# Attention scores from 64-row matmuls, the two maps on the two halves of the array's rows

## The chip, the cores and the metric

The kernel runs on one core of a Trainium2 chip. The metric is the device time of one execution, in microseconds (us). Before the change three runs gave 1631.43, 1632.15 and 1634.57 us, a median of 1632.15 us. Times inside an execution come from one profiled execution of the kernel before.

## What is computed

One layer of a hybrid encoder on 1024 tokens of width 1024, in float32. The change is in the differential attention branch: 4 heads, each with two score maps (m = 0 and 1) over 64-wide queries and keys, and one 128-wide value. Cut to that, the reference is:

```python
qa = apply_rope(qa.reshape(B, S, DA_HEADS, 2, DA_QK_DIM), cos, sin)
ka = apply_rope(ka.reshape(B, S, DA_HEADS, 2, DA_QK_DIM), cos, sin)
...
s = jnp.einsum('bqhmd,bkhmd->bhmqk', q_blk, k).astype(jnp.float32) * scale
s = jnp.where(mask, s, -jnp.inf)
a = jax.nn.softmax(s, axis=-1)
w = a[:, :, 0] - lam * a[:, :, 1]
return jnp.einsum('bhqk,bkhe->bqhe', w.astype(v.dtype), v)
```

Queries go in blocks of 128, and a block sees the keys up to its own end (64-wide chunks are masked causally). An mLSTM branch, gates, an output projection, a gated MLP and a per-layer embedding follow; the change does not touch them.

## The kernel before, in words

**Precision.** TensorE works on float32 operands that are rounded on entry (type fp32r), so each operand x is split into a rounded part hi and a rest lo = x - hi, and a product is the sum of three matmuls, hi·hi + hi·lo + lo·hi. `split` (L119) makes the two parts: hi on ScalarE (L121), lo on VectorE (L122). A 1024-deep projection is `gemm_part` (L144): per 128 rows of depth, three matmuls (L150, L151, L152) of 128 columns of weights by 512 tokens.

**The attention stage.** It runs from about 62 to 345 us of the span. Per head `make_q`, `make_k` and `make_va` (L594 to L623) project the queries, keys and values, 8 steps of 6 matmuls each. `rope_evict` (L572) takes a projected half (512 tokens) from PSUM, swaps its 32-row groups with four small DMAs on SP's queue (L581), and turns it (L582 to L584, VectorE). Rows 0 to 63 of the result (`UP`) belong to map 0 and rows 64 to 127 (`DN`) to map 1. The inner functions `parts` then split it:

- Queries: q0 holds the hi part of map 0 on the upper rows and its lo part on the lower rows, q1 the same for map 1 the other way round (L599 to L602: two ScalarE copies and two VectorE subtractions of 64 partitions for each half).
- Keys: k0 holds map 0's hi part on both halves of the rows, k1 map 1's, and kl both lo parts (L612 to L617: two ScalarE copies, two VectorE copies, two VectorE subtractions for each half).

So one 128-row matmul gives hi·hi + lo·hi of one map, and one 64-row matmul with kl gives hi·lo:

```python
PE.matmul(o, qs[h][m][:, qc], kk[m][:, n0:n1], start=True, stop=False)
PE.matmul(o, qs[h][m][r, qc], kl[r, n0:n1], start=False, stop=True)
```

These are L656 and L657 in `scores`. `weights(h, qb)` (L647) calls it for a block of 128 queries with nk = (qb+1)·128 keys, in chunks of up to 512 keys. Blocks with nk of 512 or less (qb 0 to 3) write both maps into one PSUM tile of two banks (`big`, of which there are two). Wider blocks (qb 4 to 7) take one such tile for each map, the second after the first map's scores. Then come the mask (L667, L680), the row maximum (L668, L681) on VectorE and the exponential with its row sum on ScalarE (L660). `transposed` (L687) joins the two maps (L694), turns them over on TensorE (L700) and copies them out (L701); `values` (L704) multiplies by the values (L708).

**What sets the order.** The loop at L733 writes a block's scores one block ahead of its transposes and values, and pulls single projection steps of the following heads (and later of the mLSTM values, `ps_v`) between them: one after the scores, two after the transposes. This written order gives the priorities; the framework that builds the program then arranges each engine's queue, and an instruction whose buffer or operand is not ready lets others pass it at build time. On the chip each engine keeps the order that came out. Queries and keys live in a ring of nine [128 x 1024] buffers (`qk_tile`, `NQK`), five of them for a head.

Of the kernel before, what the change touches and what calls it, by code (L numbers as in the profile page):

```python
# [11 lines left out]
F32 = mybir.dt.float32  # L12
F32R = mybir.dt.float32r
AF = mybir.ActivationFunctionType
ALU = mybir.AluOpType
# [7 lines left out]
HALF = 512  # L23
# [46 lines left out]
def block_kernel(ctx: ExitStack, tc: tile.TileContext, a: dict, out: bass.AP):  # L70
    nc = tc.nc
    PE, ACT, DVE, POOL, SP = nc.tensor, nc.scalar, nc.vector, nc.gpsimd, nc.sync
# [37 lines left out]
    def big(name):  # L110
        return pools["big"].tile([P, S], F32, tag="big", name=name)
# [7 lines left out]
    def split(hi, lo, src, scale=None, lo_eng=None):  # L119
        if scale is None:  # L120
            ACT.activation(out=hi, in_=src, func=AF.Copy)  # L121
            (lo_eng or DVE).tensor_tensor(out=lo, in0=src, in1=hi.bitcast(F32), op=ALU.subtract)  # L122
        else:
            ACT.activation(out=hi, in_=src, func=AF.Copy, scale=scale)
            DVE.scalar_tensor_tensor(
                out=lo, in0=src, scalar=scale, in1=hi.bitcast(F32), op0=ALU.mult, op1=ALU.subtract)
# [112 lines left out]
    def z_tile(t, name, evict):  # L239

        if t in ahead:
            for half, ps in enumerate(ahead.pop(t)):
                evict(half, half_slice(half), ps)
            return
        load_z(t)
        w = z_w.pop(t)
        z_order.remove(t)
        wide = big(name) if t == T_VA else None
        for half in range(2):
            if half and z_order:  # L250
                load_z(z_order[0])
            c = half_slice(half)
            ps = acc(name) if wide is None else wide[:, c]
            for k in range(0, KD, Z_STEP):
                last = k + Z_STEP == KD
                gemm_part(w[k:k + Z_STEP], cut(xg[k:k + Z_STEP], c), ps, first=k == 0, last=last)
                if last:
                    evict(half, c, ps)
                yield
# [286 lines left out]
    with tc.tile_pool(name="att", bufs=1) as at:  # L546
# [20 lines left out]
        UP, DN = slice(0, 64), slice(64, 128)  # L567

        def qk_tile(name):
            return at.tile([P, S], F32R, tag="qk", name=name, bufs=NQK)  # L570
# [15 lines left out]

            return evict

        def sub(out, in0, in1, eng=DVE):
            eng.tensor_tensor(out=out, in0=in0, in1=in1.bitcast(F32), op=ALU.subtract)  # L590

        qs, ks, vas = {}, {}, {}

        def make_q(h):  # L594

            q0, q1 = qs[h] = qk_tile("q0"), qk_tile("q1")

            def parts(rt, c):
                ACT.activation(out=q0[UP, c], in_=rt[UP, c], func=AF.Copy)  # L599
                ACT.activation(out=q1[DN, c], in_=rt[DN, c], func=AF.Copy)  # L600
                sub(q0[DN, c], rt[UP, c], q0[UP, c])
                sub(q1[UP, c], rt[DN, c], q1[DN, c])  # L602

            yield from z_tile(T_Q + h, "ps_q", rope_evict(0.125, parts))

        def make_k(h):

            k0, k1, kl = qk_tile("k0"), qk_tile("k1"), qk_tile("kl")
            ks[h] = (k0, k1), kl

            def parts(rt, c):
                ACT.activation(out=k0[UP, c], in_=rt[UP, c], func=AF.Copy)  # L612
                ACT.activation(out=k1[DN, c], in_=rt[DN, c], func=AF.Copy)
                DVE.tensor_copy(out=k0[DN, c], in_=k0[UP, c].bitcast(F32))
                DVE.tensor_copy(out=k1[UP, c], in_=k1[DN, c].bitcast(F32))
                sub(kl[UP, c], rt[UP, c], k0[UP, c])
                sub(kl[DN, c], rt[DN, c], k1[DN, c])  # L617

            yield from z_tile(T_K + h, "ps_k", rope_evict(1.0, parts))

# [24 lines left out]
        acc4 = []  # L645
        if True:
            def weights(h, qb):  # L647
                kk, kl = ks[h]
                nk = (qb + 1) * P
                qc = slice(qb * P, (qb + 1) * P)  # L650
                rs = at.tile([P, 2], F32, tag="rsum", name="rsum", bufs=3)
                nm = at.tile([P, 2], F32, tag="nmax", name="nmax", bufs=3)

                def scores(o, m, n0, n1):
                    r = (UP, DN)[m]
                    PE.matmul(o, qs[h][m][:, qc], kk[m][:, n0:n1], start=True, stop=False)  # L656
                    PE.matmul(o, qs[h][m][r, qc], kl[r, n0:n1], start=False, stop=True)  # L657

                def expo(m, e, s_):
                    ACT.activation(out=e, in_=s_, func=AF.Exp, bias=nm[:, m:m + 1], scale=1.0,  # L660
                                   accum_out=rs[:, m:m + 1])

                if nk <= HALF:
                    ps = big("ps_s").rearrange("p (m k) -> p m k", m=2)
                    for m in range(2):
                        scores(ps[:, m, 0:nk], m, 0, nk)
                    DVE.memset(ps[0:CHUNK, :, nk - CHUNK:nk], NEG)  # L667
                    DVE.tensor_reduce(out=nm, in_=ps[:, :, :nk], axis=AX.X, op=ALU.max, negate=True)  # L668
                    et = at.tile([P, S], F32, tag="e", name="e", bufs=4)
                    es = [et[:, 0:nk], et[:, HALF:HALF + nk]]  # L670
                    for m in range(2):
                        expo(m, es[m], ps[:, m, :nk])
                else:
                    es = []
                    for m in range(2):
                        ps = big("ps_s")
                        for n0 in range(0, nk, HALF):
                            n1 = min(nk, n0 + HALF)
                            scores(ps[:, n0:n1], m, n0, n1)
                        DVE.memset(ps[0:CHUNK, nk - CHUNK:nk], NEG)  # L680
                        DVE.tensor_reduce(out=nm[:, m:m + 1], in_=ps[:, :nk], axis=AX.X, op=ALU.max, negate=True)  # L681
                        et = at.tile([P, S], F32, tag="e", name="e", bufs=4)
                        expo(m, et[:, :nk], ps[:, :nk])
                        es.append(et[:, :nk])
                return es, rs

            def transposed(es, rs, qb):  # L687

                rr = at.tile([P, 2], F32, tag="rr", name="rr", bufs=3)
                DVE.reciprocal(out=rr, in_=rs)  # L690
                cc = at.tile([P, 1], F32, tag="cc", name="cc", bufs=3)
                DVE.scalar_tensor_tensor(out=cc, in0=rs[:, 0:1], scalar=neglam, in1=rr[:, 1:2],
                                         op0=ALU.mult, op1=ALU.mult)
                DVE.scalar_tensor_tensor(out=es[0], in0=es[1], scalar=cc, in1=es[0], op0=ALU.mult, op1=ALU.add)  # L694
                wT = at.tile([P, S], F32, tag="wT", name="wT", bufs=2)
                for j0 in range(0, qb + 1, 4):
                    j1 = min(qb + 1, j0 + 4)
                    pt = mid("pt")
                    for j in range(j0, j1):
                        PE.transpose(pt[:, (j - j0) * P:(j - j0 + 1) * P], es[0][:, j * P:(j + 1) * P], ident)  # L700
                    ACT.activation(out=wT[:, j0 * P:j1 * P], in_=pt[:, :(j1 - j0) * P], func=AF.Copy)  # L701
                return es, rr, wT

            def values(h, qb, es, rr, wT):  # L704
                va = vas[h]
                pav = mid("pav")
                for j in range(qb + 1):
                    PE.matmul(pav[:, :P], wT[:, j * P:(j + 1) * P], va[:, j, :], start=(j == 0), stop=(j == qb))  # L708

                i = qb % 4  # L710
                if i == 0:
                    acc4[:] = [at.tile([P, 4, P], F32, tag="oh", name="oh", bufs=2),
                               at.tile([P, 4], F32, tag="s2", name="s2", bufs=2)]
                oh, s2 = acc4
                DVE.tensor_scalar(out=oh[:, i, :], in0=pav[:, :P], scalar1=rr[:, 0:1], scalar2=None, op0=ALU.mult)
                ACT.activation(out=es[0][:, 0:P], in_=oh[:, i, :], func=AF.Square, accum_out=s2[:, i:i + 1])
                if i == 3:
                    tails.append((h, oh, s2, qb // 4))
                if tails and i == 1:
                    norm_tail(*tails.pop())  # L720
# [73 lines left out]
    def work(name, w=S, dtype=F32):  # L794
        return mw.tile([P, w], dtype, tag="m", name=name)
# [187 lines left out]
    for n, j in enumerate(OUT_ORDER):  # L983
        i = j % 4
        m = work("mg")
# [4 lines left out]
        if n % 2 == 0:  # L990
            k1 = m
# [242 lines left out]
    with tc.tile_pool(name="fin", bufs=2) as fp:  # L1234
# [25 lines left out]
        for t0, t1 in PLE_CHUNKS:  # L1260
            n = t1 - t0
            c = slice(t0, t1)
# [109 lines left out]
```

## Time and profile before

| what | value |
|---|---|
| median of three runs | 1632.15 us |
| the profiled execution's own time | 1633.46 us |
| its span, first to last instruction | 1631.6 us |
| VectorE busy | 1253.8 us (77%) |
| ScalarE busy | 730.1 us (45%) |
| GpSimd busy | 23.4 us (1%) |
| weight loads of TensorE (PEld) busy | 1284.6 us (79%) |
| mean granted clock of TensorE | 0.984 |

Busy time counts an engine's own work, not what it waits for. Matmul records overlap in the pipeline, so TensorE's pace is better read from start to start than from the length of a record. A weight load (PEld) normally runs while the matmul before it streams. In a timeline row, the bracket at the end gives the idle time in front of the instruction and what ended it; "issue" means that nothing in the profile shows what it waited for.

### The profile page before, as it was taken

How to read it: one execution, taken by the hardware profiler on the slowest of the kernel's cores; microseconds unless marked ns; L12 is line 12 of the kernel's file. 1: busy time of each engine (PE TensorE's matmuls, PEld its weight loads, DVE VectorE, ACT ScalarE, POOL GpSimd, SP SyncE). 2: the span in 40 equal slices, each digit the busy share in tenths (PEclk: the TensorE clock that was granted, in tenths of full speed). 3: DMA queues.
4: the chain of work that ended last, by engine and by line, in shares of the span. 5: the costliest groups of instructions: out<-in, count | busy, mean ns of one | idle time of the engine just before them, and what ended most of it. 6: DMA issues, size and time to landing. Idle time of an engine off the chain costs nothing.

```text
span 1631.6 us, 20986 instructions
## 1 busy us (share of the span) xinstructions
PE 1576.9 (97%) x7317; PEld 1284.6 (79%) x7317; DVE 1253.8 (77%) x2208; ACT 730.1 (45%) x1412; POOL 23.4 (1%) x22
## 2 busy tenths in 40 slices
PE   8999999998899999998998999999999989999997
PEld 7767777776787788887886788888888768788997
DVE  6687685576878878759869978877787897878745
ACT  3354453554464664543446433333333544343522
POOL 0000000000000000000000000000000000000000
PEclk8999999999999999999999999999999999999998
DMA  5212121063334232355413332333333654442422
GB/s 187 72 27 71 40 71 41 27 222 117 125 102 127 81 131 92 117 191 164 155 47 134 110 103 98 103 107 101 102 106 102 207 182 148 143 134 58 133 83 91
DMA packets 97882, 181.62 MB, mean 111 GB/s; under 512 B 11696, under 2 KB 21488, under 8 KB 97776
## 3 DMA queue, kind: packets, MB, share of 16 engines
q1 hardware_dynamic: 97200, 179.76, 34.1%
q8 instruction: 58, 0.95, 0.2%
q10 hardware_dynamic: 576, 0.52, 0.1%
q14 instruction: 48, 0.39, 0.1%
HBM read 131.18 MB, written 44.86 MB: 108 GB/s over the span
## 4 chain that ended last, share of the span: by engine, by line
PE 64%; DVE 9%; issue 2%; DMA 2%; ACT 1%; POOL 0%; SPq 0%; POOLq 0%; DVEq 0%; ACTq 0%
PE b L376 18%; PE b L374 18%; PE b L375 18%; PE ps_pg L1272 1%; PE ps_pg L1273 1%; PE ps_pg L1274 1%; DVE cv L823 1%; DVE T L122 1%; DVE mg L292 1%; DVE wl L122 1%; DVE B L122 1%; PE ps_ya L152 1%; DVE hs L388 1%; DMA sg<-ya 1%; PE ps_ya L151 1%
## 5 line engine op out<-in xcount | busy, mean ns | idle before, releaser
L374 PE MATMUL b<-T,wh 128*128 128x512 f32 x816 | 320.0, 392 | 3.8 <-DVE x L292 1.4
L376 PE MATMUL b<-T,wl 128*128 128x512 f32 x816 | 319.8, 392 | 3.8 <-DVE wl L122 3.8
L375 PE MATMUL b<-T,wh 128*128 128x512 f32 x816 | 318.8, 391 | 0.5 <-DVE T L122 0.5
L121 ACT ACTIVATE wh<-S 128x512 fp32r<-128x512 f32 (+1 forms) x208 | 129.4, 622 | 275.6 <-PE b L375 249.1
L374 PE MATMUL b<-B,wh 128*128 128x512 f32 x612 | 240.7, 393 | 2.5 <-ACT wh L121 2.0
L376 PE MATMUL b<-B,wl 128*128 128x512 f32 x612 | 240.1, 392 | 0.6 <-DVE wl L122 0.6
L375 PE MATMUL b<-B,wh 128*128 128x512 f32 x612 | 239.8, 392 | 0.5 <-DVE B L122 0.5
L122 DVE TENSOR_TENSOR wl<-S,wh 128x512 fp32r<-128x512 f32 (+1 forms) x208 | 140.1, 674 | 61.0 <-ACT wh L121 61.0
L374 PEld LDWEIGHTS b<-T,wh 128*128 128x128 f32 x816 | 153.7, 188 | 40.4 <-DVE x L292 2.6
L376 PEld LDWEIGHTS b<-T,wl 128*128 128x128 f32 x816 | 153.8, 188 | 38.3 <-DVE wl L122 6.2
L375 PEld LDWEIGHTS b<-T,wh 128*128 128x128 f32 x816 | 153.8, 188 | 33.4 <-DVE T L122 1.6
L121 ACT ACTIVATE wh<-wr 128x512 fp32r<-128x512 f32 (+1 forms) x156 | 96.9, 621 | 166.6 <-PE b L375 151.6
L374 PEld LDWEIGHTS b<-B,wh 128*128 128x128 f32 x612 | 115.4, 189 | 27.6 <-ACT wh L121 3.3
L376 PEld LDWEIGHTS b<-B,wl 128*128 128x128 f32 x612 | 115.5, 189 | 25.4 <-DVE wl L122 1.7
L375 PEld LDWEIGHTS b<-B,wh 128*128 128x128 f32 x612 | 115.4, 189 | 25.3 <-DVE B L122 1.8
L292 DVE TENSOR_TENSOR x<-b,x 128x512 f32<-128x512 f32 x112 | 77.0, 688 | 47.9 <-PE b L376 46.4
L122 DVE TENSOR_TENSOR wl<-wr,wh 128x512 fp32r<-128x512 f32 (+1 forms) x156 | 104.9, 672 | 7.5 <-ACT wh L121 5.9
L292 DVE TENSOR_TENSOR S<-wr 128x512 f32<-128x512 f32 (+1 forms) x104 | 70.3, 676 | 1.7 <-DMA wr<-w_down 0.2
L1117 DVE SCALAR_TENSOR_TENSOR ac<-ar,vec,ac 128x511 f32<-128x511 f32 (+1 forms) x88 | 65.8, 747 | 0.7
L121 ACT ACTIVATE wh<-wf 128x512 fp32r<-128x512 f32 (+1 forms) x56 | 33.5, 601 | 63.0 <-PE ps_q L151 19.5
L1272 PE MATMUL ps_pg<-x,wpg 128*128 128x384 f32 (+1 forms) x192 | 61.3, 319 | 0.0
L1274 PE MATMUL ps_pg<-x,wpg 128*128 128x384 f32 (+1 forms) x192 | 61.0, 318 | 0.0
(305 smaller groups left out, 2794.8 us busy)
## 6 DMA issues: line engine op xcount, KB each, us to landing
wr<-w_up SPq DMA_DIRECT2D x88, 256.0 KB, 2.8
wr<-w_in SPq DMA_DIRECT2D x56, 256.0 KB, 3.0
wf<-w_in SPq DMA_DIRECT2D x32, 256.0 KB, 2.9
wr<-w_down SPq DMA_DIRECT2D x32, 256.0 KB, 2.8
xt<-xT SPq DMA_DIRECT2D x8, 512.0 KB, 6.2
sw<-raw SPq DMA_DIRECT2D x64, 64.0 KB, 2.0
hs<-xT SPq DMA_DIRECT2D x8, 512.0 KB, 5.4
ya<-ya SPq DMA_DIRECT2D x16, 256.0 KB, 2.0
```

The source lines that it names most:

```text
L121: ACT.activation(out=hi, in_=src, func=AF.Copy)
L122: (lo_eng or DVE).tensor_tensor(out=lo, in0=src, in1=hi.bitcast(F32), op=ALU.subtract)
L151: PE.matmul(ps, wh, xl, start=False, stop=False)
L152: PE.matmul(ps, wl, xh, start=False, stop=(last and k == n - 1))
L292: eng.tensor_tensor(out=out, in0=in0, in1=in1, op=op)
L374: PE.matmul(bank[b], wh, xh, start=(k == 0 and not more), stop=False, **kw)
L375: PE.matmul(bank[b], wh, xl, start=False, stop=False, **kw)
L376: PE.matmul(bank[b], wl, xh, start=False, stop=(k == n - 1), **kw)
L388: DVE.scalar_tensor_tensor(out=hs[i][:, c], in0=(src or hs)[i][:, c], scalar=v(gain, i), in1=rstd[:, c], op0=ALU.mult, op1=ALU.mult)
L1117: DVE.scalar_tensor_tensor(out=o[:, d:], in0=ar[:, j + d:j + HALF], scalar=v("cf", t * 3 + j), in1=o[:, d:], op0=ALU.mult, op1=ALU.add)
L1272: PE.matmul(pg, wh, xh[:, c], start=(i == 0), stop=False)
L1274: PE.matmul(pg, wl, xh[:, c], start=False, stop=(i == KD - 1))
```

## The change

Each of q and k is split plainly into a hi and a lo tile of 128 partitions (map 0 on the upper half, map 1 on the lower). Scores are three 64-row matmuls per map: hi·hi, hi·lo, lo·hi. They are issued in turn for the two maps, so that neighbours lie on different halves of the array's rows. A wide block asks for both PSUM tiles before its first score, and its maxima and exponentials follow after all its scores. A head now holds four ring buffers, not five. VectorE keeps all subtractions; the helper `sub` goes.

```diff
         def make_q(h):
-            q0, q1 = qs[h] = qk_tile("q0"), qk_tile("q1")
+            qh, ql = qs[h] = qk_tile("qh"), qk_tile("ql")
             def parts(rt, c):
-                ACT.activation(out=q0[UP, c], in_=rt[UP, c], func=AF.Copy)
-                ACT.activation(out=q1[DN, c], in_=rt[DN, c], func=AF.Copy)
-                sub(q0[DN, c], rt[UP, c], q0[UP, c])
-                sub(q1[UP, c], rt[DN, c], q1[DN, c])
+                split(qh[:, c], ql[:, c], rt[:, c])
...
         def make_k(h):
-            k0, k1, kl = qk_tile("k0"), qk_tile("k1"), qk_tile("kl")
-            ks[h] = (k0, k1), kl
+            kh, kl = ks[h] = qk_tile("kh"), qk_tile("kl")
             def parts(rt, c):
-                ACT.activation(out=k0[UP, c], in_=rt[UP, c], func=AF.Copy)
-                ACT.activation(out=k1[DN, c], in_=rt[DN, c], func=AF.Copy)
-                DVE.tensor_copy(out=k0[DN, c], in_=k0[UP, c].bitcast(F32))
-                DVE.tensor_copy(out=k1[UP, c], in_=k1[DN, c].bitcast(F32))
-                sub(kl[UP, c], rt[UP, c], k0[UP, c])
-                sub(kl[DN, c], rt[DN, c], k1[DN, c])
+                split(kh[:, c], kl[:, c], rt[:, c])
...
-                def scores(o, m, n0, n1):
-                    r = (UP, DN)[m]
-                    PE.matmul(o, qs[h][m][:, qc], kk[m][:, n0:n1], start=True, stop=False)
-                    PE.matmul(o, qs[h][m][r, qc], kl[r, n0:n1], start=False, stop=True)
+                def scores(o, n0, n1):
+                    terms = (qh, kh), (qh, kl), (ql, kh)
+                    for i, (q_, k_) in enumerate(terms):
+                        for m, r in enumerate((UP, DN)):
+                            PE.matmul(o[m], q_[r, qc], k_[r, n0:n1], start=(i == 0), stop=(i == len(terms) - 1))
...
                 if nk <= HALF:
                     ps = big("ps_s").rearrange("p (m k) -> p m k", m=2)
-                    for m in range(2):
-                        scores(ps[:, m, 0:nk], m, 0, nk)
+                    scores([ps[:, m, 0:nk] for m in range(2)], 0, nk)
...
                 else:
-                    es = []
-                    for m in range(2):
-                        ps = big("ps_s")
-                        for n0 in range(0, nk, HALF):
-                            n1 = min(nk, n0 + HALF)
-                            scores(ps[:, n0:n1], m, n0, n1)
+                    pss, es = [big("ps_s") for _ in range(2)], []
+                    for n0 in range(0, nk, HALF):
+                        n1 = min(nk, n0 + HALF)
+                        scores([ps[:, n0:n1] for ps in pss], n0, n1)
+                    for m, ps in enumerate(pss):
                         DVE.memset(ps[0:CHUNK, nk - CHUNK:nk], NEG)
                         DVE.tensor_reduce(out=nm[:, m:m + 1], in_=ps[:, :nk], axis=AX.X, op=ALU.max, negate=True)
```

## Rows read from the trace of the kernel before

**Rows 1.** The page, part 1: TensorE's busy time, share of the span, instructions.
```profile
PE 1576.9 (97%) x7317; PEld 1284.6 (79%) x7317; DVE 1253.8 (77%) x2208; ACT 730.1 (45%) x1412; POOL 23.4 (1%) x22
```

**Rows 2.** Windows: stretch, length, busy us by engine (instructions), granted clock, DMA.
```profile
62.00:130.00 68.00, 65.11 (x299) 47.02 (x298) 55.70 (x117) 34.04 (x85) 1.01 (x1) 0.97 0.18 51
130.00:200.00 70.00, 70.00 (x350) 53.59 (x349) 49.99 (x106) 33.86 (x87) 3.19 (x3) 1.00 0.17 46
200.00:270.00 70.00, 70.00 (x343) 52.95 (x343) 46.65 (x97) 33.84 (x83) 3.14 (x3) 1.00 0.20 61
270.00:335.00 65.00, 64.92 (x330) 48.62 (x329) 37.35 (x97) 27.62 (x70) 1.01 (x1) 1.00 0.11 33
```

**Rows 3.** Timeline of a projection on TensorE: start, length, engine, line, operation.
```profile
152.39 0.39 PE L152 MATMUL ps_k<-xh,wl 128*128 128x512 f32 x1
152.40 0.19 PEld L150 LDWEIGHTS ps_k<-xh,wh 128*128 128x128 f32 x1
...
152.62 0.40 PE L150 MATMUL ps_k<-xh,wh 128*128 128x512 f32 x1
```

**Rows 4.** Timeline of one map's scores, 512 and then 128 keys.
```profile
150.47 0.50 PE L656 MATMUL ps_s<-k,q 128*128 128x512 f32 x1
150.90 0.18 PEld L657 LDWEIGHTS ps_s<-kl,q 64*128 64x128 f32 x1 [0.24 <-issue]
150.90 0.49 PE L657 MATMUL ps_s<-kl,q 64*128 64x512 f32 x1
...
151.32 0.33 PE L656 MATMUL ps_s<-k,q 128*128 128x128 f32 x1
...
151.58 0.32 PE L657 MATMUL ps_s<-kl,q 64*128 64x128 f32 x1
...
151.83 0.50 PE L150 MATMUL ps_k<-xh,wh 128*128 128x512 f32 x1
```

**Rows 5.** The lines L656 and L657, each in its own view: counts by shape.
```profile
L656 PE MATMUL ps_s<-k,q x96: 221/430/505, 67.1 to 319.7; 128*128 128x512 f32 x48, 128*128 128x128 f32 x16, 128*128 128x256 f32 x16, 128*128 128x384 f32 x16
...
L657 PE MATMUL ps_s<-kl,q x96: 323/466/503, 67.3 to 320.1; 64*128 64x512 f32 x48, 64*128 64x128 f32 x16, 64*128 64x256 f32 x16, 64*128 64x384 f32 x16
```

**Rows 6.** Waits of TensorE's weight loads, 62 to 335 us: total, times, longest.
```profile
PEld ps_s L657 <- issue: 16.5, 65, 0.4
PEld ps_s L656 <- issue: 9.9, 42, 0.2
...
PEld ps_s L657 <- DVE kl L590: 0.4, 1, 0.4
```

**Rows 7.** Timeline: eight value matmuls of 128 columns in a row, and the next.
```profile
160.05 1.16 PE L708 MATMUL pav<-va,wT 128*128 128x128 f32 x8
...
160.96 0.48 PE L150 MATMUL ps_k<-xh,wh 128*128 128x512 f32 x1
```

**Rows 8.** Timeline: wide blocks' first scores beside the exponentials of the block before.
```profile
79.93 0.39 PE L656 MATMUL ps_s<-k,q 128*128 128x512 f32 x1
...
87.36 0.67 ACT L660 ACTIVATE e<-ps_s,nmax 128x512 f32<-128x512 f32 x1
...
285.65 0.40 PE L656 MATMUL ps_s<-k,q 128*128 128x512 f32 x1
...
286.78 0.66 ACT L660 ACTIVATE e<-ps_s,nmax 128x512 f32<-128x512 f32 x1
```

**Rows 9.** Groups by shape, and the line L615 in its own view.
```profile
L590 DVE TENSOR_TENSOR q<-raw,q 64x512 fp32r<-64x512 f32 x16 | 11.0, 686 | 2.3 <-ACT q L599 1.9
...
L122 DVE TENSOR_TENSOR wl<-wf,wh 128x512 fp32r<-128x512 f32 x40 | 27.1, 684 | 14.0 <-ACT wh L121 14.0
...
L615 DVE CAST k<-k x8: 421/422/424, 66.9 to 240.7; 64x512 fp32r<-64x512 f32 x8
```

**Rows 10.** Timeline of the stage's end: the last values, and the next stage's first matmul.
```profile
333.23 1.95 PE L708 MATMUL pav<-va,wT 128*128 128x128 f32 x16
...
345.21 0.40 PE L150 MATMUL ps_ya<-hi,wh 128*128 128x512 f32 x1
```

More of the change, by code (lines that the diff above doesn't have):

```diff
@@ L587, in rope_evict @@
             return evict
-        def sub(out, in0, in1, eng=DVE):
-            eng.tensor_tensor(out=out, in0=in0, in1=in1.bitcast(F32), op=ALU.subtract)
         qs, ks, vas = {}, {}, {}
         def make_q(h):
-            q0, q1 = qs[h] = qk_tile("q0"), qk_tile("q1")
+            qh, ql = qs[h] = qk_tile("qh"), qk_tile("ql")
             def parts(rt, c):
-                ACT.activation(out=q0[UP, c], in_=rt[UP, c], func=AF.Copy)
-                ACT.activation(out=q1[DN, c], in_=rt[DN, c], func=AF.Copy)
-                sub(q0[DN, c], rt[UP, c], q0[UP, c])
-                sub(q1[UP, c], rt[DN, c], q1[DN, c])
+                split(qh[:, c], ql[:, c], rt[:, c])
             yield from z_tile(T_Q + h, "ps_q", rope_evict(0.125, parts))
         def make_k(h):
-            k0, k1, kl = qk_tile("k0"), qk_tile("k1"), qk_tile("kl")
-            ks[h] = (k0, k1), kl
+            kh, kl = ks[h] = qk_tile("kh"), qk_tile("kl")
             def parts(rt, c):
-                ACT.activation(out=k0[UP, c], in_=rt[UP, c], func=AF.Copy)
-                ACT.activation(out=k1[DN, c], in_=rt[DN, c], func=AF.Copy)
-                DVE.tensor_copy(out=k0[DN, c], in_=k0[UP, c].bitcast(F32))
-                DVE.tensor_copy(out=k1[UP, c], in_=k1[DN, c].bitcast(F32))
-                sub(kl[UP, c], rt[UP, c], k0[UP, c])
-                sub(kl[DN, c], rt[DN, c], k1[DN, c])
+                split(kh[:, c], kl[:, c], rt[:, c])
             yield from z_tile(T_K + h, "ps_k", rope_evict(1.0, parts))
@@ L647, in weights @@
             def weights(h, qb):
-                kk, kl = ks[h]
+                (qh, ql), (kh, kl) = qs[h], ks[h]
                 nk = (qb + 1) * P
```

## The prediction, made before the changed kernel was run

> **What bounds the kernel now.** I read the page first: TensorE is busy for 97% of the span [rows 1], so a change counts by what it does to TensorE's queue. Then the windows of the attention stage: of the 273 us from 62 to 335 TensorE's records fill 270.0 (65.11 + 70.00 + 70.00 + 64.92), with VectorE at 189.7 and ScalarE at 129.4 [rows 2]. A busy TensorE may still go slowly, so the third view is the timeline, read from start to start. A projection matmul of 512 columns follows the last one after 0.23 us, and the weights of the next load while it streams: the load at 152.40 lies right behind the start at 152.39 [rows 3]. In the scores this is lost. A 128-row matmul of 512 columns is followed by its 64-row partner 0.43 us later, and that by the next 128-row one 0.42 us later; at 128 columns the steps are 0.26 and 0.25 [rows 4]. So whenever the number of rows changes, the next load waits until the stream is over and about 0.2 us stand bare, whatever the width. The waits view books this as "issue", 16.5 us ahead of L657 and 9.9 us ahead of L656 [rows 6]. There are 192 score matmuls, and each one is followed by such a change [rows 5].
>
> **What the scores cost now.** Call a chunk one group of up to 512 keys of both maps: two L656 and two L657. By the counts there are 24 chunks of 512 keys and 8 each of 384, 256 and 128 [rows 5]. A step costs 0.425 us at 512 columns and 0.255 at 128 [rows 4]; on a line between, 0.368 at 384 and 0.312 at 256. A chunk is four steps: 1.70, 1.47, 1.25, 1.02 us. Sum: 24 x 1.70 + 8 x (1.47 + 1.25 + 1.02) = 70.7 us.
>
> **What they cost after.** A chunk is six 64-row matmuls, three for each half of the rows. The number of rows changes twice per chunk, not four times: once going in (0.2 us more on the matmul before) and once going out (the last step at 0.425, 0.368, 0.312 or 0.255). Between them lies what the trace does not show: 64-row matmuls on different halves, side by side. Bounds: a pair takes one stream, 0.23 us at 512 columns, or two, 0.46. I take one, since the nearest row is the 128-row matmul [rows 3]: a pair streams the same 128 partitions through the same 128 rows. For narrow pairs the loads set the pace: eight load-and-matmul steps of 128 columns took 0.91 us, 0.11 each [rows 7], so a pair needs 0.22. The second half starts between 0 and 0.11 us behind the first; I take 0.05. A 512 chunk is then 0.20 + 2 x 0.228 + 0.05 + 0.425 = 1.13 us, and with 0.22 a pair the others are 1.06, 1.00 and 0.945. Sum: 24 x 1.13 + 8 x 3.005 = 51.1 us, **19.6 us less**.
>
> The Trainium skill has a price for such packing (TensorE: Matmul & The Clock Gate, "Measured speedup vs the span model"): four 32-row tiles of 512 columns ran 3.07 times as fast as one after another, that is, in 1.3 streams. If a pair took 1.3 streams too, an estimate from that page, 48 pairs of 512 columns ahead of the last would cost 0.07 us more each and the gain would be some 3 us smaller. No row here shows it.
>
> **Chunks of one block side by side.** 16 blocks have two chunks. Where both stand together in the queue, one going out and one going in fall away, 0.4 us: 0 to 6.4 us. I take half, **3.2 us less**, since the build may put a projection step between.
>
> **The new wait.** A wide block now needs both PSUM tiles before its first score; before, map 0 started when one was free. Behind that score stands all of TensorE's queue; the maxima and exponentials of both maps wait for it. In 7 of the 16 wide blocks the first score came ahead of the end of the exponentials of the block before: first at 79.93, with an exponential running until 88.03, last at 285.65, with one until 287.44 [rows 8]; the seven lags add up to 18 us. They cost nothing as long as projection steps stand in between, as TensorE's 65.11 of 68 us in the very stretch of the longest one shows [rows 2]. Also, map 0's maximum now starts after map 1's scores. Bounds 0 and 18 us; I take **4 us more**, nearer the covered end because most of the lag is in head 0, where three heads' steps are left to fill with.
>
> **What I cost at nothing.** VectorE loses 16 subtractions of 0.686 us (one of 128 partitions takes no longer, 0.684) and 16 copies of 0.422, 17.7 us in all [rows 9]; ScalarE loses 16 of its 32 copies here. Both are hidden by TensorE, and less of them makes the cover safer. Four buffers per head instead of five fit twice into the ring of nine; the wait for the lo keys is 0.4 us now [rows 6], and I leave it. No DMA is added, removed or moved past another. After the last values TensorE still has projection steps until the next stage starts at 345.21, some 10 us of it [rows 10]; if the attention chain lags by that much at the end, they cover it. The later stages just start earlier.
>
> Sum: -19.6 - 3.2 + 4 = -18.8 us. On the profiled execution's own 1633.46 us (span 1631.6) that is 1614.7; it stands 1.3 above the median, so on the median I forecast 1613.5 us. Its own range: both chunks always adjacent, no lag of the second half and no wait gives -28 us, 1604; waits of 12 us and no adjacency give -8, 1624.
>
> **Rivals.**
> *A half waits for its own stream.* The next load for the upper rows may not start while those rows stream, so each half goes at 0.425 a step, both halves at once. A 512 chunk is 0.20 + 2 x 0.425 + 0.05 + 0.425 = 1.525, the others 1.354, 1.186, 1.015: 65.0 us, 5.7 less; adjacency saves only 0.2 each (1.6 by half), the wait costs 4: about 1629 us. Against it: 128-row loads do go in behind a stream of the same rows [rows 3]. For it: no 64-row load here ever did. The Trainium skill says (same page, "The mechanism") that a load overlaps a running matmul only when the row groups differ; read strictly it gives this rival, and the trace's 128-row stream contradicts the strict reading. Chance 0.10.
>
> *No side by side.* The halves go one after the other but loads keep up: 512: 0.20 + 5 x 0.228 + 0.425 = 1.765; the others 1.418, 1.097, 1.005: 70.5 us. Nothing gained but adjacency, minus the wait: +0.6, about 1633 us. That is the change not doing what it says. Chance 0.10.
>
> *Slower: every change of half is paid like a change of rows.* If the bare 0.2 us comes with any new row group, all six matmuls pay it: 0.20 + 6 x 0.425 = 2.75, the others 2.41, 2.07, 1.73: 115.7 us, +45, less 1.6: about 1675 us. For it: every 64-row score in the trace pays it. Against: each of them follows or precedes a matmul that shares its rows; two halves share none. It decides as soon as a pair at 512 columns takes over about 0.5 us. The Trainium skill is against it (TensorEngine Tiling (Array Packing), "Key Properties"): only a change of tiling mode drains the engine, not a change of tile. Chance 0.12.
>
> **How the numbers follow.** Forecast 0.68, rivals 0.10, 0.10, 0.12. A measurement here tells 0.2%, 3.3 us, from no change. Faster: nearly all of the forecast, half of the first rival, a little of the second: 0.74. Same: half of the second rival, part of the first: 0.09. Slower: 0.17. The range 1604 to 1632 holds the forecast, the first rival and half of the second, a little under 0.8.
>
> **What would show it.** Right: score matmuls of the two maps start in pairs within 0.11 us, pairs 0.23 us apart at 512 columns; two bare loads per group instead of one per matmul; ps_ya's first matmul near 326 us instead of 345.21; from there on the same stages. The forecast is wrong if starts within a group are even at 0.23 (second rival) or 0.42 (third), if each half repeats at 0.42 (first), or if TensorE shows idle time ahead of the scores with the exponential (L660 before) as releaser, of more than 12 us in all.

## The result, and the profile after

Four runs of the changed kernel gave 1610.4 to 1614.45 us, median 1612.03, beside 1633.36 for the kernel before on the same chip: a ratio of 0.9865, 95% interval 0.9849 to 0.9881, 21.3 us faster. The forecast was 1613.5 us, 18.8 us faster. The profiled execution took 1610.4 us with a span of 1608.6.

First the page of the changed kernel, part 1, and its windows of the attention stage, to be held against [rows 1] and [rows 2]. The stage now ends at 325 us, so the last window is 55 us long.

```profile
PE 1548.1 (96%) x7413; PEld 1274.6 (79%) x7413; DVE 1238.0 (77%) x2176; ACT 718.9 (45%) x1396; POOL 23.4 (1%) x22
```

```profile
62.00:130.00 68.00, 66.78 (x377) 51.48 (x376) 52.83 (x114) 33.65 (x89) 2.42 (x2) 1.00 0.20 55
130.00:200.00 70.00, 68.45 (x409) 55.96 (x408) 51.71 (x108) 34.93 (x92) 2.01 (x2) 1.00 0.22 62
200.00:270.00 70.00, 66.84 (x368) 52.02 (x364) 46.24 (x114) 29.25 (x75) 2.92 (x3) 0.98 0.17 51
270.00:325.00 55.00, 53.79 (x317) 43.22 (x317) 30.47 (x65) 25.86 (x61) 2.53 (x2) 1.00 0.19 64
```

TensorE is still the engine that is busy, but its records no longer fill the windows: 3.2 us are free between 200 and 270, where none were before. The granted clock is no term of the difference: its mean over the stage is 0.99 in both kernels, and in each some 3 us run at 0.50, the lower of the two levels (1.2 GHz), after TensorE had stood partly idle (before from about 73 us, with 3.1 of the 4 us from 68 to 72 busy; after from 216.8 us, with 1.7 of the 4 us from 212 to 216 busy).

Next the timeline of TensorE in one wide block of the changed kernel (768 keys: a chunk of 512 and one of 256), with the start of the stage behind it. "x2" means that two matmuls of the same kind, here one of each map, stand in one row. Where the row is as long as one matmul (0.40 us at 512 columns), they start together; in this kernel's records map 1's start lies 0.003 us behind map 0's (median of the pairs of 512 columns). Line numbers are those of each run's own kernel.

```profile
147.28 0.50 PE L646 MATMUL ps_s<-kh,qh 64*128 64x512 f32 x2
147.62 0.40 PE L646 MATMUL ps_s<-kl,qh 64*128 64x512 f32 x2
147.85 0.39 PE L646 MATMUL ps_s<-kh,ql 64*128 64x512 f32 x2
148.08 0.28 PE L646 MATMUL ps_s<-kh,qh 64*128 64x256 f32 x2
148.20 0.28 PE L646 MATMUL ps_s<-kl,qh 64*128 64x256 f32 x2
148.32 0.28 PE L646 MATMUL ps_s<-kh,ql 64*128 64x256 f32 x2
148.53 0.50 PE L150 MATMUL ps_k<-xh,wh 128*128 128x512 f32 x1
148.87 0.40 PE L151 MATMUL ps_k<-xl,wh 128*128 128x512 f32 x1
...
324.85 0.40 PE L150 MATMUL ps_ya<-hi,wh 128*128 128x512 f32 x1
```

Pairs of 512 columns follow each other after 0.23 us, pairs of 256 after 0.12, across the two chunks without a break. What a change of rows costs stands at both ends, about half ahead of the change and half behind it. Behind it, the first pair is followed after 0.34 instead of 0.23, and so is the first 128-row matmul behind the group (148.53 to 148.87). Ahead of it, the last pair is followed after 0.21 instead of 0.12 (148.32 to 148.53). In [rows 4] every single score matmul paid both halves, 0.2 us. The next stage starts at 324.85 us where it started at 345.21 [rows 10], 20.4 us sooner; the first score is 0.9 us later than before (68.06 for 67.13), so from the first score to the end of the stage it is 256.8 us where it was 278.1.

Last the waits of TensorE's weight loads from 62 us to the end of the stage, against [rows 6]. Columns: total, times, longest.

```profile
PEld ps_s L646 <- ACT e L649: 5.6, 6, 1.7
PEld ps_s L646 <- issue: 3.8, 17, 0.4
PEld pav L695 <- ACT wT L688: 2.3, 7, 0.5
...
PEld pt L277 <- ACT wT L688: 2.2, 5, 0.7
```

The bare loads ahead of scores fell from 26.4 us (16.5 + 9.9) to 3.8. In exchange TensorE waits for others. Summed over all rows of this view that name another engine, it is 15.2 us where the kernel before had 5.9, each up to the end of its stage. The largest, 5.6 us, is the wait for both PSUM tiles: the exponentials of the block before.

### The profile page after: what moved, and what is told of

Read it like the earlier page. It is cut to its first block, busy times and chain, and to the rows that moved or that the text cites. A ratio compares the mean times of both kernels' runs of the same rounds, so it can differ in the third digit from the quotient of the medians.

```text
span 1608.6 us, 21129 instructions
## 1 busy us (share of the span) xinstructions
PE 1548.1 (96%) x7413; PEld 1274.6 (79%) x7413; DVE 1238.0 (77%) x2176; ACT 718.9 (45%) x1396; POOL 23.4 (1%) x22
## 4 chain that ended last, share of the span: by engine, by line
PE 63%; DVE 10%; DMA 3%; issue 3%; ACT 1%; POOL 0%; SPq 0%; POOLq 0%; DVEq 0%; ACTq 0%
PE b L376 18%; PE b L374 17%; PE b L375 17%; PE ps_pg L1259 2%; PE ps_pg L1260 2%; PE ps_pg L1261 1%; DVE T L122 1%; DVE cv L810 1%; DVE mg L292 1%; DVE wl L122 1%; DVE B L122 1%; PE ps_ya L152 1%; DVE hs L388 1%; PE ps_ya L151 1%; PE ps_ya L150 1%
## 5 line engine op out<-in xcount | busy, mean ns | idle before, releaser
L649 ACT ACTIVATE e<-ps_s,nmax 128x128 f32<-128x128 f32 (+7 forms) x64 | 47.1, 737 | 35.9 <-DVE nmax L668 21.9
```

## The experiments

Each ran beside the kernel before on the same chip, and ratios are to that kernel; the changed kernel's is 0.9865. Differences in us from the changed kernel are the difference of the ratios times 1633; such a difference carries both intervals, some 4 to 6 us either way, so where it is small the stage in the trace is read beside it.

### 1. The order of a chunk's six matmuls

```diff
-                    for i, (q_, k_) in enumerate(terms):
-                        for m, r in enumerate((UP, DN)):
+                    for m, r in enumerate((UP, DN)):
+                        for i, (q_, k_) in enumerate(terms):
```

> The changed kernel with only the order of the six matmuls of a chunk altered: the three of map 0, then the three of map 1, so that neighbours mostly share a half of the rows. Theory (two halves run as one stream, which is where most of the gain over serial 64-row matmuls comes from): a chunk takes five streams instead of three, because only the last of map 0 and the first of map 1 lie side by side: 24 x 2 x 0.23 + 8 x 2 x (0.175 + 0.12 + 0.11) = 17 us more, less up to 3 us where the last of map 1 lies beside the first of the next chunk: 1626 to 1629 us. Rival 1 (only the fewer changes of the number of rows count): no change from the changed kernel, 1612 us. Rival 2 (a half cannot load behind its own stream): steps of 0.42 us within a map, over 1640 us.

Measured: 1611.88 us, ratio 0.9865 (0.9843 to 0.9888), the same as the changed kernel. The number is rival 1's, the reason is not. TensorE's queue as built, for one chunk of 256 keys, three matmuls of map 0 and then three of map 1:

```
L646 MATMUL ps_s<-kh,qh 128x256
L646 MATMUL ps_s<-kl,qh 128x256
L646 MATMUL ps_s<-kh,ql 128x256
L646 MATMUL ps_s<-kh,qh 128x256
L646 MATMUL ps_s<-kl,qh 128x256
L646 MATMUL ps_s<-kh,ql 128x256
```

And the timeline of this kernel, same block as above:

```profile
148.83 0.50 PE L646 MATMUL ps_s<-kh,qh 64*128 64x512 f32 x2
149.16 0.40 PE L646 MATMUL ps_s<-kl,qh 64*128 64x512 f32 x2
149.40 0.40 PE L646 MATMUL ps_s<-kh,ql 64*128 64x512 f32 x2
149.62 0.29 PE L646 MATMUL ps_s<-kh,qh 64*128 64x256 f32 x2
```

Map 1's first matmul is fourth in the queue and starts with the first, by the records 0.010 us behind it (median of the pairs of 512 columns), where it was 0.003 with the maps in turn. So the pairs form again, whatever the written order: the matmul of the other half goes past two of the first half that have not run. The experiment could not take the pairs away, and says nothing on what they are worth. Number 2 does.

### 2. Both maps on one half

```diff
-                            PE.matmul(o[m], q_[r, qc], k_[r, n0:n1], ...
+                            PE.matmul(o[m], q_[UP, qc], k_[UP, n0:n1], ...
```

> The changed kernel with both maps read from the upper 64 rows, so that map 1's scores are computed from map 0's queries and keys and the lower half of the array's rows lies idle: the same matmuls, chunks and tiles, but nothing can run side by side. Theory (the two halves run as one stream): 24 x 3 x 0.23 + 8 x 3 x (0.175 + 0.12 + 0.11) = 26 us more of TensorE, of which up to 8 us swallow waits: 1630 to 1638 us. Rival (only the fewer changes of the number of rows count): 1612 us.

Measured: 1627.96 us, ratio 0.9959 (0.9943 to 0.9974): 15.4 us above the changed kernel. The timeline of the same block:

```profile
153.52 0.73 PE L646 MATMUL ps_s<-kh,qh 64*128 64x512 f32 x2
154.08 0.62 PE L646 MATMUL ps_s<-kl,qh 64*128 64x512 f32 x2
154.55 0.62 PE L646 MATMUL ps_s<-kh,ql 64*128 64x512 f32 x2
155.01 0.39 PE L646 MATMUL ps_s<-kh,qh 64*128 64x256 f32 x2
155.25 0.39 PE L646 MATMUL ps_s<-kl,qh 64*128 64x256 f32 x2
```

Here the two of a row run one after the other: the row is 0.62 us long, and not 0.40. Two matmuls now take 0.46 to 0.47 us, and 0.24 at 256 columns: twice the stream. Side by side is worth this difference. It is also seen that a half does load behind its own stream, or the steps would be 0.42 each as in [rows 4]; that settles the first rival. The waits for other engines fall to 6.3 us from 15.2, so of 26 us of added streams 9 are swallowed; the 17 that remain stand beside 15.4 measured (15.6 in the trace, from the first score to the end of the stage). The time is a little under the 1630 to 1638 expected, as the waits swallowed somewhat more than the 8 us allowed for.

### 3. More changes of the number of rows

One 128-row matmul of 64 columns with zero weights in every chunk, which adds nothing to the sums:

```diff
+        none = at.tile([P, P], F32R, tag="none", name="none")
+        DVE.memset(none.bitcast(F32), 0.0)
...
                     for i, (q_, k_) in enumerate(terms):
+                        if i == 1:
+                            PE.matmul(o[0][:, 0:64], none, kh[:, n0:n0 + 64], start=False, stop=False)
                         for m, r in enumerate((UP, DN)):
```

> The changed kernel with one extra 128-row matmul of 64 columns in every chunk, ahead of its second pair (zero weights, added to the first 64 columns of map 0, so the sums do not change): two more changes of the number of rows in each of 48 chunks. Theory (a change costs 0.2 us bare): 48 x (0.2 + 0.2 + 0.03) = 21 us more than the changed kernel, about 1632 us, with 5 us less of it where waits are swallowed: 1627 to 1634. Rival (changes of rows are not what the scores paid for; the saving is in the streams): within 4 us of the changed kernel.

Measured: 1628.42 us, ratio 0.9956 (0.9935 to 0.9977): 14.9 us above the changed kernel. The timeline of the same block:

```profile
149.84 0.50 PE L650 MATMUL ps_s<-kh,qh 64*128 64x512 f32 x2
150.26 0.30 PE L648 MATMUL ps_s<-kh,none 128*128 128x64 f32 x1
150.49 0.50 PE L650 MATMUL ps_s<-kl,qh 64*128 64x512 f32 x2
150.82 0.40 PE L650 MATMUL ps_s<-kh,ql 64*128 64x512 f32 x2
```

From the first to the third pair it takes 0.98 us, against 0.57 in the changed kernel: 0.41 us for two changes, as forecast (0.43). 48 of them make 19.7 us, and the waits for other engines fall from 15.2 to 7.9 us, which leaves 12.4. From the first score to the end of the stage the trace shows 11.9 us more (66.0 to 334.7, against 68.1 to 324.8). The other 3 us of the median lie in stages that the edit does not touch and stay open.

### 4. The block structure alone

The kernel before with both PSUM tiles asked for first, scores chunk by chunk, and maxima after all scores:

```diff
-                    es = []
-                    for m in range(2):
-                        ps = big("ps_s")
-                        for n0 in range(0, nk, HALF):
-                            n1 = min(nk, n0 + HALF)
-                            scores(ps[:, n0:n1], m, n0, n1)
+                    pss, es = [big("ps_s") for _ in range(2)], []
+                    for n0 in range(0, nk, HALF):
+                        n1 = min(nk, n0 + HALF)
+                        for m in range(2):
+                            scores(pss[m][:, n0:n1], m, n0, n1)
+                    for m, ps in enumerate(pss):
```

> The kernel before with only the block structure of the change: a wide block asks for both PSUM tiles before its first score, scores go chunk by chunk, and both maxima come after all scores. The matmuls stay as they were. Theory (the new wait costs about 5 us, as the trace of the changed kernel shows with the exponential as releaser): 3 to 6 us slower than the kernel before. Rival (the wait is covered by projection steps): within 1.5 us of the kernel before.

Measured: 1635.37 us, ratio 1.0005 (0.9993 to 1.0018). My theory falls, the rival stands: with the old matmuls the new wait is fully covered, its view of waits shows 6.0 us for other engines as against 5.9. So the 5.6 us behind the exponentials in the changed kernel are not the price of the structure by itself. They come with the shorter scores: in numbers 2 and 3, whose scores take longer, the same wait is 0.8 and 1.4 us.

### 5. The old splits, whole and in parts

In the prediction the relief of VectorE and ScalarE was worth nothing. First all of it is put back, with the new matmuls: 64-row splits, and copies of the hi keys into a fifth ring tile kx that the first product reads.

```diff
-                split(qh[:, c], ql[:, c], rt[:, c])
+                for r in (UP, DN):
+                    split(qh[r, c], ql[r, c], rt[r, c])
...
-                split(kh[:, c], kl[:, c], rt[:, c])
+                for r in (UP, DN):
+                    split(kh[r, c], kl[r, c], rt[r, c])
+                    DVE.tensor_copy(out=kx[r, c], in_=kh[r, c].bitcast(F32))
...
-                    terms = (qh, kh), (qh, kl), (ql, kh)
+                    terms = (qh, kx), (qh, kl), (ql, kh)
```

> The changed kernel with the old load on the other engines: splits done in 64-row halves and two 64-row copies of the hi keys into a fifth ring tile that the first product reads. 16 more operations on ScalarE, 16 more subtractions and 16 copies on VectorE, five buffers per head. Theory (these were hidden before and are worth nothing): within 3 us of the changed kernel, 1609 to 1615 us. Rival (the relief of VectorE, ScalarE and the ring is part of the gain): 4 us or more above the changed kernel.

Measured: 1620.46 us, ratio 0.9919 (0.9890 to 0.9948), 8.8 us above the changed kernel. The theory falls. Two reasons were left: the ring and the engines' load. The ring first, from both sides: seven buffers in the changed kernel (`NQK = 7`), and ten with the old splits (`NQK = 10`).

> The changed kernel with a ring of seven buffers for its queries and keys instead of nine: four per head and seven in all are one short, as five per head and nine were before; no operation differs. Theory A (the run with the old splits was slower because of the load on VectorE and ScalarE): within 3 us of the changed kernel. Theory B (because the ring holds back the next head's keys): 5 to 9 us slower than the changed kernel, 1617 to 1621 us.

Measured: 1612.76 us, ratio 0.9868 (0.9851 to 0.9885).

> The run with the old splits (16 more operations on ScalarE, 16 more subtractions and 16 copies on VectorE, five buffers per head) with a ring of ten buffers, which holds two heads. Theory A (the load on VectorE and ScalarE costs): 1617 to 1622 us, as with nine buffers. Theory B (the ring costs): 1610 to 1615 us, as the changed kernel.

Measured: 1618.30 us, ratio 0.9905 (0.9890 to 0.9920). No cost of the ring can be told either way; the load costs 6.5 us with ten buffers. Then the load engine by engine. ScalarE's part alone (`halves` stands in the place of `split` for queries and keys):

```diff
+        def halves(hi, lo, src):
+            for r in (UP, DN):
+                ACT.activation(out=hi[r], in_=src[r], func=AF.Copy)
+            DVE.tensor_tensor(out=lo, in0=src, in1=hi.bitcast(F32), op=ALU.subtract)
```

> The changed kernel with ScalarE's part of the old splits alone: the hi part in two 64-row halves, 16 operations of 0.63 us more, on the way to each lo part; VectorE and the ring as in the change. The old splits as a whole cost some 7 us, with either ring. Theory S (ScalarE's 10 us cost, by the later copies and exponentials behind them): 4 to 7 us above the changed kernel, 1616 to 1619 us. Theory V (VectorE's 17.7 us cost): within 2 us of the changed kernel.

Measured: 1609.15 us, ratio 0.9847 (0.9817 to 0.9876): no cost. VectorE's part alone has `ACT.activation` on all 128 rows, the subtraction in two halves, and the copies into kx:

> The changed kernel with VectorE's part of the old splits alone: the lo part in two 64-row halves, and two 64-row copies of the hi keys into a fifth ring tile that the first product reads; 16 subtractions and 16 copies more, 17.7 us. Theory V (VectorE's load costs): 4 to 7 us above the changed kernel, 1616 to 1619 us. Theory S (ScalarE's load costs): within 2 us of the changed kernel.

Measured: 1619.80 us, ratio 0.9906 (0.9874 to 0.9939), 6.7 us above the changed kernel; the intervals just touch, but the stage ends at 331.98, 7.1 us later. From the first score to the end of the stage the three kernels with VectorE's load need 6.7, 7.2 and 6.1 us more than the changed kernel (whole, ten buffers, VectorE's part), and the one with ScalarE's part 2.8 us less. So it is VectorE's load. The waits of this kernel from 62 to 332 us show how it arrives at TensorE:

```profile
PEld pav L702 <- ACT wT L695: 6.0, 13, 1.1
...
PEld pt L277 <- ACT wT L695: 2.9, 5, 1.1
PEld pt L694 <- DVE e L688: 2.0, 2, 1.0
PEld ps_s L653 <- ACT e L656: 1.8, 5, 0.5
```

The same view of the kernel with ScalarE's part, from 62 to 323.7 us, has these two rows:

```profile
PEld pav L700 <- ACT wT L693: 6.0, 10, 2.1
...
PEld ps_s L651 <- ACT e L654: 0.7, 2, 0.4
```

The values (pav) wait 6.0 us for the copies behind the transposes, where the changed kernel has 2.3. This alone is not it, since with ScalarE's part the wait is as large; there the scores wait less in exchange, 0.7 us for 5.6, and the stage is not longer. With VectorE's part the scores wait less too, but the transposes wait 2.0 us for the join of the two maps (L688, VectorE), and the scores 0.9 us for the copies into kx. In all TensorE waits 18.1 us for other engines, against 12.6 with ScalarE's part, and its waits marked "issue" are 15.7 us against 12.7. VectorE is busy 198 of 270 us there, far from full; that the place of the join in its queue counts, and not the sum of its work, is my reading, which no run tested by itself.

### 6. More relief for VectorE

If VectorE's load costs when added, does taking more away gain? Two ways were tried. The lo parts of the projection weights on GpSimd:

```diff
-            z_w[t] = load_w(a["w_in"][t], 0, KD)
+            z_w[t] = load_w(a["w_in"][t], 0, KD, lo_eng=POOL)
```

> The changed kernel with the lo parts of the projection weights made on GpSimd, not on VectorE: some 25 subtractions of 0.68 us, 17 us, leave VectorE in this stage. Theory V (with TensorE faster, VectorE's queue sets the waits that are left, 12 us behind exponentials and copies whose maxima and joins VectorE makes): 2 to 6 us faster than the changed kernel, 1606 to 1610 us. Rival (GpSimd is slower at it, delays the weights, or slows VectorE beside it): the same or slower.

Measured: 1616.62 us, ratio 0.9891 (0.9863 to 0.9918), not clearly off the changed kernel; the stage ends 4.0 us later, at 328.80. Of these, 3.1 us are lost ahead of the first score (at 71.2, against 68.1); from there to the end of the stage it is 0.9 us more. Two groups of this kernel's trace (mean ns behind the busy time) show what stands against a gain:

```profile
L122 POOL TENSOR_TENSOR wl<-wf,wh 128x512 fp32r<-128x512 f32 x24 | 38.2, 1593 | 184.8 <-ACT wh L121 184.8
```

```profile
L583 DVE TENSOR_TENSOR sw<-sw,tab_s 128x512 f32<-128x512 f32 x14 | 10.7, 763 | 0.0
```

A subtraction takes 1593 ns on GpSimd, against 684 on VectorE [rows 9], and VectorE's own multiplications in the same stretch rise to 763 ns; in the changed kernel the same 14 took 682. Then the scaling of a block's values on ScalarE, whose spare time the run above had shown:

```diff
-                DVE.tensor_scalar(out=oh[:, i, :], in0=pav[:, :P], scalar1=rr[:, 0:1], scalar2=None, op0=ALU.mult)
+                ACT.activation(out=oh[:, i, :], in_=pav[:, :P], func=AF.Copy, scale=rr[:, 0:1])
```

> The changed kernel with the scaling of a block's values (32 times a 128x128 tile out of PSUM, 0.35 us each, 11.1 us) moved from VectorE to ScalarE, whose own 16 extra operations cost nothing in an earlier run. Theory V (VectorE's queue sets the waits left in the stage; 17.7 us more on it cost about 8 us): 2 to 5 us faster than the changed kernel, 1607 to 1610 us. Rival (VectorE has been relieved enough by the change and more relief is worth nothing): within 2 us of the changed kernel; or ScalarE's queue, now longer ahead of its copies, makes it slower.

Measured: 1610.43 us, ratio 0.9851 (0.9831 to 0.9870): 2.3 us under the changed kernel, inside its interval. By the time alone the theory and the first rival cannot be told apart. In the trace the stage is not shorter (257.3 us from the first score to its end, for 256.8), and the wait behind the exponentials is 5.7 us for 5.6. So the first rival is the nearer one: 11 us moved from VectorE to ScalarE buy nothing that can be told.

### 7. No 64-row matmuls at all

```diff
-            k0, k1, kl = qk_tile("k0"), qk_tile("k1"), qk_tile("kl")
-            ks[h] = (k0, k1), kl
+            k0, k1, l0, l1 = (qk_tile(n) for n in ("k0", "k1", "l0", "l1"))
+            ks[h] = (k0, k1), (l0, l1)
...
-                sub(kl[UP, c], rt[UP, c], k0[UP, c])
-                sub(kl[DN, c], rt[DN, c], k1[DN, c])
+                sub(l0[UP, c], rt[UP, c], k0[UP, c])
+                sub(l1[DN, c], rt[DN, c], k1[DN, c])
+                DVE.tensor_copy(out=l0[DN, c], in_=l0[UP, c].bitcast(F32))
+                DVE.tensor_copy(out=l1[UP, c], in_=l1[DN, c].bitcast(F32))
...
-                    PE.matmul(o, qs[h][m][r, qc], kl[r, n0:n1], start=False, stop=True)
+                    PE.matmul(o, qs[h][m][:, qc], kl[m][:, n0:n1], start=False, stop=True)
```

> The kernel before with its 64-row matmul made a 128-row one: the lo keys of each map stand on both halves of the rows (two tiles l0, l1 instead of kl, so lo times lo is added as well), ring of ten buffers. No change of rows is left in the scores and nothing runs side by side. Theory (each change of the number of rows stands bare for 0.2 us): a chunk is 4 streams: 24 x 0.91 + 8 x (0.70 + 0.48 + 0.44) = 35 us of TensorE against 70.7 before and some 45 after; VectorE has 6.8 us more than before, hidden; six buffers per head in a ring of ten make the next head's lo keys wait for this head's last scores, up to 2 us three times: 1598 to 1608 us. Rival (the gain of the change needs the two halves side by side, or the ring and VectorE bind): 1612 us or more.

Measured: 1612.93 us, ratio 0.9861 (0.9832 to 0.9890), the same as the changed kernel, and the expectation of 1598 to 1608 missed. The streams did get cheap: in the timeline of its first 512-key chunk the steps are as in a projection once the first load is in:

```profile
74.73 0.50 PE L657 MATMUL ps_s<-k,q 128*128 128x512 f32 x1 [2.42 <-ACT e L661]
75.06 0.39 PE L658 MATMUL ps_s<-l,q 128*128 128x512 f32 x1
75.30 0.39 PE L657 MATMUL ps_s<-k,q 128*128 128x512 f32 x1
75.53 0.41 PE L658 MATMUL ps_s<-l,q 128*128 128x512 f32 x1
```

So the gain of the change can be had without two halves side by side: it is the changes of rows that the kernel before paid for. The stage ends at 321.32, 3.5 us sooner than with the change, but 1.4 us of this lie ahead of the first score (66.7 for 68.1). From the first score to the end it is 2.2 us less (254.6 for 256.8), where I had expected 10 us of saved streams. Those 10 were too many: by the terms measured below, the scores of the changed kernel cost 39.8 us (70.7 - 30.9), not 45, so 35 is 4.8 us less. Waits for other engines take 3.2 us of it back, 18.4 for 15.2, the longest of them the one in the bracket above; this leaves 1.6, beside the 2.2. VectorE has 201 us of work in the stage, against 181; whether this makes the waits, as in number 5, was not tried. The rest of the lead is lost between 404 and 694 us, in work that the edit does not touch: 2.4 us of it in waits of TensorE for one VectorE operation (kw, two waits of 3.9 us together, for 1.5 in the changed kernel). Why they are longer is not explained.

## Why the prediction was right, point by point

**TensorE sets the stage's time.** Right: the next stage was expected near 326 us and starts at 324.85.

**A pair takes one stream.** Right for 512 columns, 0.23 us. For narrow pairs the term was mis-sized: I let the loads of the two halves go one after the other, 0.22 us a pair, and 0.05 us of lag per chunk. Inside a group, pairs of 384, 256 and 128 columns follow each other after 0.175, 0.12 and 0.11 us (medians of the trace), and the lag is 0.003; the loads of both halves go together. That is 16 x (0.045 + 0.10 + 0.11) = 4.1 us, and the lag 48 x 0.05 = 2.4 us. **Chunks side by side:** 12 of the 16 wide blocks kept all 12 matmuls in one group, not half of them: 1.6 us more. The scores' terms should have been -30.9 us, not -22.8.

**The new wait.** Taken at 4 us, and nearly right: the scores' wait for the exponentials grew from 0.8 to 5.6 us, by 4.8, inside the bounds of 0 and 18. In the kernel before, up to the end of the stage, it was:

```profile
PEld ps_s L656 <- ACT e L660: 0.8, 2, 0.5
```

My reason for a low value, that steps fill the lag, held with the old scores (number 4) and not once they were short. The other waits for other engines, which the sum does not have at all, grew by 4.5 us more (5.1 to 9.6). -30.9 + 4.8 + 4.5 = -21.6 us, beside 21.3 from the first score to the end of the stage, 20.4 at the end of the stage and 21.3 in the medians. That the forecast came within 3 us was luck: 8.1 us of gain and 5.3 us of waits were missing from it, and they cancelled.

**What I cost at nothing.** This step failed. "Both are hidden by TensorE, and less of them makes the cover safer": the second half of the sentence was the thing to price. With the old splits under the new matmuls the gain is 13.2 us (0.9919), so 6.5 to 8.8 of the 21.3 us hang on VectorE's relief (the three runs of number 5: 8.8, 6.5, 6.7). They stand in no term of the sum: without the relief the waits would have grown by more. No gain from ScalarE's relief or from the ring can be told, as forecast.

**The rivals.** A half that waits for its own stream is refuted in number 2. No side by side is refuted by the rows of the result: the matmuls of a pair start together, and the next pair follows after 0.23 us, where one half alone takes 0.46 for two (number 2). Every change of half paid like a change of rows is refuted by the same rows, since pairs of both halves run through at 0.23.

## What to carry to other kernels

Read TensorE from start to start: in this kernel each change of the number of rows costs 0.2 us above the stream, a price per change, and it can be saved by grouping as well as by filling up to 128 rows. Work that is hidden has a price as soon as its cover is cut, so when an edit shortens the bounding engine by some per cent, price the chains behind it again at the new pace. Terms that cancel show only in the waits, so a sum that fits is no proof of its parts.

## What was not expected of the hardware

Matmuls on different halves of the rows need not be neighbours in the queue: in number 1 one that stood fourth started 0.01 us behind the first. So what stands above on the kernel before, that on the chip each engine keeps the order that came out, does not hold for TensorE here. The Trainium skill (TensorE: Matmul & The Clock Gate, "The mechanism") says that matmuls start in program order and only loads are pulled ahead; these rows differ, and the measurement decides. The passing has a limit, seen in a block of the changed kernel whose second PSUM tile came late:

```profile
154.72 0.50 PE L646 MATMUL ps_s<-kh,qh 64*128 64x512 f32 x1
156.64 0.50 PE L646 MATMUL ps_s<-kh,qh 64*128 64x512 f32 x1 [1.42 <-ACT e L649]
156.64 0.72 PE L646 MATMUL ps_s<-kl,qh 64*128 64x512 f32 x2
```

Map 0's first matmul ran at 154.72. Its second, next but one in the queue, did not pass map 1's first, which waited for the exponential; both started at 156.64. With the maps one after the other (number 1), the three of map 0 ran ahead of that wait in the same block. How far ahead TensorE looks was not tried.
